# Gate rows built in token pairs instead of token eights (one inference step with a PEER expert mixer)

## Chip, cores and metric

The kernel runs on one core of one Trainium2 chip. The metric is the device time of one execution in microseconds (us), the median of several runs.

## What is computed

One step of a small decoder layer for 512 prompt tokens and 32 sample tokens, 1024 wide: retention heads and a convolution, an output projection, a norm, then PEER, an expert mixer whose experts are single neurons, and a second norm. The part that the change touches is PEER. In the reference it is, for a block of tokens:

```python
v1, i1 = lax.top_k(s1, PEER_TOPK)          # 16 of 128 first keys, per head
v2, i2 = lax.top_k(s2, PEER_TOPK)          # 16 of 128 second keys
cand = v1[..., :, None] + v2[..., None, :]
sv, ci = lax.top_k(cand, PEER_TOPK)        # 16 pairs of keys
e1, e2 = ...                               # first and second key of each pair
idx = e1 * N_KEYS + e2                     # one of 128*128 experts
gate = jax.nn.softmax(sv)
u = jnp.take(peer_u, idx, axis=0)
act = jax.nn.gelu(jnp.einsum('phkd,pd->phk', u, xb), approximate=False)
vv = jnp.take(peer_v, idx, axis=0)
out = jnp.einsum('phk,phkd->pd', gate * act, vv)
```

There are 8 heads with 16 pairs each, so every token chooses 128 of 16,384 experts.

## The kernel before, in words

The tokens are treated in two ways. Some 288 of them (128 prompt tokens at first, the 32 samples, 128 more prompt tokens) **gather** the rows of their experts by indirect DMA: `gather` (L566 to L577) fetches one expert row per token, 128 tokens at a time (1 MB), VectorE multiplies it with the token (L569), ScalarE makes the weight (L571, L572), and VectorE adds the weighted row (L577). The other 256 tokens (`ND`) are treated **densely**: all 128 x 128 experts are scored on TensorE, one second key `e` (128 experts) at a time. `scores_of(e)` loads 512 KB of u and makes eight products, two passes each in the trace (L776, tile `sp`). A table of gates with an entry for every token and expert, most of them zero, is multiplied by the gelu of these scores. `v_stage(e)` then multiplies the result with 512 KB of v into the accumulators `pB` (L907). The table lies in four parts by second key: Gb holds keys 0 to 31, Gc 32 to 51, Ga 52 to 95, Gd 96 to 127 (`EG`, `E0S`).

The table of gates is made by **`build`**, eight tokens (`TB`) to a pass, 256 / 8 = 32 passes to a call. For a token, the partitions are its 128 (head, pair) slots. Matrix A has a one where a slot's first key is `e1`; it is made on ScalarE, per token an absolute difference to a row 0..127 (`off`, L850, eight instructions), then one Relu over the eight tokens (L852). Matrix M has a one where the slot's second key is `e2` (L854, VectorE, one instruction for eight tokens). B is M times the gate of the slot; the gate is split into three bfloat16 parts `gtT[:, q]`, so that B has three parts (L857, one VectorE instruction). For each token three bfloat16 products of A (stationary, 128 columns) and a column set of B (moving, `ne` columns) add up in one PSUM tile: 24 products and 24 weight loads a pass (L863). A result covers `nt` tokens.

`build` is called twice. **`first_keys`** covers the keys 0 to 95 (`ne` = 96, `nt` = 4). For each four tokens VectorE multiplies the PSUM result into Gb and Ga, and into the finished part of Gc (L887), and copies the rest of Gc (L889). In between, `s_stage` scores one key of Gc after every 12 tokens (L871 to L874). **`last_keys`** covers the keys 96 to 127 (`ne` = 32, `nt` = 16); ScalarE copies its result into Gd. It runs later, between the `v_stage`s.

M, B and A have two buffers each, `off` one, the PSUM tiles `mm` and `sp` two each. B is laid out as `[3, ne, TB]`: the eight tokens are innermost, so one token's columns lie 8 elements, 16 bytes, apart:

```python
B = bt.tile([128, 3, ne, TB], BF, name="B")
T.matmul(pt[:, t % nt], A[:, t - t1], B[:, q, :, t - t1], ...)
```

The constant `iot` holds the key numbers, each repeated for the eight tokens, made once by GpSimd at the start (L171).

The order of the instructions on each engine is fixed when the program is built: a scheduler places them by a timeline of its own. Each engine then executes its list in order, and waits on semaphores. In the built order, the 32 passes of `first_keys` stand on TensorE between score products of Gb and Gc: about one key's scores follow each pass, and the last eight passes (192 products) stand without any.

Of the kernel before, what the change touches and what calls it, by code (L numbers as in the profile page):

```python
# [10 lines left out]
BF = mybir.dt.bfloat16  # L11
# [3 lines left out]
OP = mybir.AluOpType  # L15
# [9 lines left out]
PH, NK, TK = 8, 128, 16  # L25
# [6 lines left out]
TB = 8  # L32
# [59 lines left out]
def tile_step(ctx: ExitStack, tc: tile.TileContext, a, o):  # L92
    nc = tc.nc
    V, S, T, G = nc.vector, nc.scalar, nc.tensor, nc.gpsimd

    per = ctx.enter_context(tc.tile_pool(name="per", bufs=1))
# [15 lines left out]
    def mmps():  # L112
        turn[0] += 1
        return banks[turn[0] % len(banks)].tile([128, 512], F32, name="mm")
# [7 lines left out]
    def cc(n):  # L122
        part, c, w = COFF[n]
        return cst[part][:, c:c + w]
# [42 lines left out]
    def small(name, shape, dt=F32, bufs=2):  # L167
        return wk.tile(shape, dt, name=name, bufs=bufs)

    iot = per.tile([128, NK, TB], BF, name="iot")  # L170
    G.iota(iot, pattern=[[1, NK], [0, TB]], base=0, channel_multiplier=0, allow_small_or_imprecise_dtypes=True)  # L171
    row = per.tile([128, NK], BF, name="row")
    G.iota(row, pattern=[[1, NK]], base=0, channel_multiplier=0, allow_small_or_imprecise_dtypes=True)
    mhalf = per.tile([128, 1], F32, name="mhalf")
# [25 lines left out]
    def rope(w, blk, xT, n, col0, outs):  # L200

        def turn_head(h):
            pm = mmps()
            for c0, c1, dst in outs:
                A = dst[:, h]
                T.matmul(pm[:, c0:c1], perm, A, start=True, stop=True)
                B = small("ropeB", [128, 416], bufs=1)[:, :c1 - c0]
                V.tensor_mul(B, pm[:, c0:c1], cc("sin")[:, col0 + c0:col0 + c1])
                V.tensor_mul(A, A, cc("cos")[:, col0 + c0:col0 + c1])
                V.tensor_add(A, A, B)  # L210

# [400 lines left out]
    e2T = per.tile([128, ND], BF, name="e2T")  # L612
    gtT = per.tile([128, 3, ND], BF, name="gtT")
# [183 lines left out]
    for g in range(2):  # L797
# [9 lines left out]
        p = mmps().rearrange("p (q t) -> p q t", q=4)  # L807
# [32 lines left out]
            residual(pB[b][q], x1T, range(q * 4, q * 4 + 4), NG2 + b * 128)  # L840
    GW[1] = gc.tile([128, EG[1], ND], F32, name="Gc")

    def build(bt, e0, ne, nt):


        pt = None
        for t1 in range(0, ND, TB):
            off = bt.tile([128, TB, NK], BF, name="off", bufs=1)
            for t in range(TB):
                S.activation(off[:, t], row, AF.Abs, bias=e1T[:, t1 + t:t1 + t + 1])  # L850
            A = bt.tile([128, TB, NK], BF, name="A")
            S.activation(A, off, AF.Relu, bias=1.0, scale=-1.0)  # L852
            M = bt.tile([128, ne, TB], BF, name="M")
            V.tensor_tensor(M, iot[:, e0:e0 + ne],  # L854
                            e2T[:, t1:t1 + TB].unsqueeze(1).to_broadcast([128, ne, TB]), op=OP.is_equal)
            B = bt.tile([128, 3, ne, TB], BF, name="B")
            V.tensor_tensor(B, M.unsqueeze(1).to_broadcast([128, 3, ne, TB]),  # L857
                            gtT[:, :, t1:t1 + TB].unsqueeze(2).to_broadcast([128, 3, ne, TB]), op=OP.mult)
            for t in range(t1, t1 + TB):
                if t % nt == 0:  # L860
                    pt = pdn.tile([128, nt, ne], F32, name="mm")
                for q in range(3):
                    T.matmul(pt[:, t % nt], A[:, t - t1], B[:, q, :, t - t1], start=(q == 0), stop=(q == 2))  # L863
                if t % nt == nt - 1:
                    yield pt, slice(t - nt + 1, t + 1)

# [9 lines left out]
    def first_keys():  # L876

        with tc.tile_pool(name="bt", bufs=2, reuse_waits="tile") as bt:
            done = 0
            for pt, ts in build(bt, 0, E0S[3], 4):  # L880
                for g, e0, e1, ready in ((0, 0, EG[0], True), (2, 0, EG[2], True), (1, 0, done, True), (1, done, EG[1], False)):
                    if e0 == e1:
                        continue
                    to = GW[g][:, e0:e1, ts]
                    part = pt[:, :, E0S[g] + e0:E0S[g] + e1].rearrange("p t e -> p e t")
                    if ready:
                        V.tensor_mul(to, to, part)  # L887
                    else:
                        V.tensor_copy(to, part)  # L889
                if ts.stop % 12 == 0 and done < EG[1]:  # L890
                    s_stage(E0S[1] + done, ts.stop)
                    done += 1

    def last_keys():

        with tc.tile_pool(name="bt", bufs=2, reuse_waits="tile") as bt:
            for pt, ts in build(bt, E0S[3], EG[3], 16):
                S.activation(GW[3][:, :, ts], pt.rearrange("p t e -> p e t"), AF.Copy)
                yield
# [53 lines left out]
    for b in range(2):  # L953
        t = uvp.tile([128, D], F32, name="uv")
# [50 lines left out]
```

## Time and profile before

| | |
|---|---|
| median of 3 runs | 1742.75 us (1738.49 to 1743.54) |
| profiled execution: its time, its span | 1744.1 us, 1742.3 us |
| mean granted TensorE clock in it | 0.943 |
| busy: TensorE, VectorE, ScalarE, GpSimd | 94%, 72%, 35%, 22% |
| HBM traffic | 503 MB, 289 GB/s over the span |

Busy shares are those of the profiled execution, against its span. A matmul's duration contains its passage through the array, and the next one starts before it ends; the distance from one to the next is what the engine spends on it. Granted clock is the share of full TensorE speed that the chip's throttle gave in that stretch.

### The profile page before, as it was taken

How to read it: one execution, taken by the hardware profiler on the slowest of the kernel's cores; microseconds unless marked ns; L12 is line 12 of the kernel's file. 1: busy time of each engine (PE TensorE's matmuls, PEld its weight loads, DVE VectorE, ACT ScalarE, POOL GpSimd, SP SyncE). 2: the span in 40 equal slices, each digit the busy share in tenths (PEclk: the TensorE clock that was granted, in tenths of full speed). 3: DMA queues.
4: the chain of work that ended last, by engine and by line, in shares of the span. 5: the costliest groups of instructions: out<-in, count | busy, mean ns of one | idle time of the engine just before them, and what ended most of it. 6: DMA issues, size and time to landing. Idle time of an engine off the chain costs nothing.

```text
span 1742.3 us, 20660 instructions
## 1 busy us (share of the span) xinstructions
PE 1635.5 (94%) x7014; PEld 1111.1 (64%) x7014; DVE 1250.1 (72%) x3037; ACT 603.4 (35%) x1687; POOL 375.6 (22%) x335
## 2 busy tenths in 40 slices
PE   7899899969599889999999999999999999999997
PEld 6887566547465578887877666544557665553443
DVE  4949899898658989999566776776665777776201
ACT  1324441452212323334334555541688211111000
POOL 1002222345222222200210110232222422222000
PEclk9899999979799999999998887699999999999998
DMA  9469679978987689955965551499988999999642
GB/s 361 156 211 363 251 257 336 346 266 280 370 322 260 243 317 355 357 190 168 354 251 194 184 202 37 159 415 423 395 291 309 359 424 424 423 424 424 213 154 99
DMA packets 99542, 503.75 MB, mean 289 GB/s; under 512 B 10183, under 2 KB 21191, under 8 KB 56549
## 3 DMA queue, kind: packets, MB, share of 16 engines
q0 software_dynamic: 42240, 305.12, 45.8%
q1 hardware_dynamic: 50749, 189.96, 29.4%
q10 hardware_dynamic: 6448, 7.36, 1.3%
q8 instruction: 55, 0.90, 0.2%
q14 instruction: 50, 0.41, 0.1%
HBM read 497.03 MB, written 5.80 MB: 289 GB/s over the span
## 4 chain that ended last, share of the span: by engine, by line
PE 58%; DVE 21%; DMA 14%; issue 4%; POOL 2%; ACT 1%; SPq 0%; DVEq 0%; POOLq 0%; ACTq 0%
PE pB L907 22%; PE sp L776 15%; PE mm L863 9%; DMA g<-in_uv_dram,I 7%; PE mm L196 5%; DVE acc L577 4%; DVE g L569 4%; PE mm L306 2%; DMA uv<-in_ut_dram 2%; PE mm L261 2%; DMA g<-in_uv_dram,Ib 2%; DMA g<-in_w_in_dram 1%; POOL g L566 1%; DVE oh L546 1%; DMA out_dram<-keys 1%
## 5 line engine op out<-in xcount | busy, mean ns | idle before, releaser
L776 PE MATMUL sp<-x1T,uv 128*128 128x256 f32 x2048 | 485.5, 396 | 19.4 <-ACT Ga L822 7.2
L776 PEld LDWEIGHTS sp<-x1T,uv 128*128 128x128 f32 x2048 | 403.0, 200 | 101.9 <-issue 25.1
L577 DVE SCALAR_TENSOR_TENSOR acc<-g,wgt,acc 128x1024 f32<-128x1024 f32 x285 | 365.1, 1281 | 93.9 <-ACT wgt L572 92.7
L566 POOL DMA_INDIRECT g<-in_uv_dram,I x128 | 167.6, 1310 | 437.3 <-DVE acc L577 228.1
L569 DVE SCALAR_TENSOR_TENSOR g<-g,x1g 128x1024 f32<-128x1024 f32 x160 | 195.3, 1223 | 68.1 <-DMA g<-in_uv_dram,Ib 60.5
L566 POOL DMA_INDIRECT g<-in_uv_dram,Ib x128 | 143.6, 1122 | 406.1 <-DVE acc L577 360.3
L571 ACT ACTIVATE act<-act 128x1 f32<-128x1 f32 x288 | 57.4, 200 | 493.8 <-DVE g L569 493.4
L863 PE MATMUL mm<-B,A 128*128 128x96 bf16 (+1 forms) x1536 | 188.5, 294 | 5.1 <-DVE Gc L889 3.8
L569 DVE SCALAR_TENSOR_TENSOR g<-g,x 128x1024 f32<-128x1024 f32 x128 | 155.8, 1217 | 40.2 <-DMA g<-in_uv_dram,I 38.4
L196 PE MATMUL mm<-x1T,w 128*128 128x384 f32 (+1 forms) x512 | 179.5, 505 | 3.3 <-ACT score L522 2.6
L863 PEld LDWEIGHTS <-A 128*128 128x128 bf16 x1536 | 139.2, 117 | 65.5 <-issue 19.8
L907 PE MATMUL pB<-uv,Ga 128*128 128x512 f32 x352 | 162.3, 604 | 1.1 <-DMA uv<-in_uv_dram 0.8
L850 ACT ACTIVATE off<-row,e1T 128x128 bf16<-128x128 bf16 x512 | 157.8, 388 | 4.0 <-PE mm L863 3.0
L196 PEld LDWEIGHTS mm<-x1T,w 128*128 128x128 f32 x512 | 96.9, 192 | 76.0 <-issue 40.4
L907 PE MATMUL pB<-uv,Gb 128*128 128x512 f32 x256 | 119.9, 622 | 0.4 <-DVE Gb L887 0.4
L907 PEld LDWEIGHTS pB<-uv,Ga 128*128 128x128 f32 x352 | 63.8, 190 | 82.8 <-issue 62.6
L907 PE MATMUL pB<-uv,Gd 128*128 128x512 f32 x256 | 110.1, 593 | 0.1
L852 ACT ACTIVATE A<-off 128x1024 bf16<-128x1024 bf16 x64 | 67.4, 1054 | 97.7 <-PE mm L863 97.3
L907 PEld LDWEIGHTS pB<-uv,Gb 128*128 128x128 f32 x256 | 49.6, 200 | 61.7 <-issue 54.3
L857 DVE TENSOR_TENSOR B<-M,gtT 128x2304 bf16<-128x2304 bf16 (+1 forms) x64 | 60.8, 953 | 38.3 <-PE mm L863 38.3
L907 PEld LDWEIGHTS pB<-uv,Gd 128*128 128x128 f32 x256 | 48.6, 190 | 61.5 <-issue 60.4
L566 POOL DMA_INDIRECT g<-in_uv_dram,Is x32 | 36.0, 1126 | 210.8 <-DVE acc L577 115.5
(277 smaller groups left out, 1787.0 us busy)
## 6 DMA issues: line engine op xcount, KB each, us to landing
uv<-in_ut_dram SPq DMA_DIRECT2D x128, 512.0 KB
uv<-in_uv_dram SPq DMA_DIRECT2D x128, 512.0 KB
w<-in_w_in_dram SPq DMA_DIRECT2D x18, 1024.0 KB
w<-in_w_query_dram SPq DMA_DIRECT2D x16, 1024.0 KB
w<-in_w_out_dram SPq DMA_DIRECT2D x7, 1024.0 KB
g<-in_uv_dram,I POOLq DMA_INDIRECT x128, 7.9
keys<-in_state_retention_dram ACTq DMA_DIRECT2D x4, 512.0 KB
out_dram<-keys SPq DMA_DIRECT2D x4, 512.0 KB
```

Source lines behind the costliest of these rows:

```text
L196: T.matmul(p[:, :n], w[m // 2][:, k, (m % 2) * 128:(m % 2 + 1) * 128], xT[:, k, c0:c0 + n], start=(k == 0), stop=(k == 7))
L261: T.matmul(p[:, :L], dg[:, k % 4], u_p[:, m, p0 + k:p0 + k + L], start=(k == 0), stop=(k == CK - 1))
L566: G.indirect_dma_start(out=t, out_offset=None, in_=a["uv"], in_offset=bass.IndirectOffsetOnAxis(ap=idx[:, k:k + 1], axis=0))
L569: V.scalar_tensor_tensor(t[:, :D], t[:, :D], 1.0, x1, op0=OP.mult, op1=OP.mult, accum_out=act[:, 0:1])
L571: S.activation(act[:, 1:2], act[:, 0:1], AF.Gelu)
L577: V.scalar_tensor_tensor(acc, v, wgt, acc, op0=OP.mult, op1=OP.add)
L776: T.matmul(sp, u[:, k], x1T[:, k, NG2:], start=(k == 0), stop=(k == 7))
L850: S.activation(off[:, t], row, AF.Abs, bias=e1T[:, t1 + t:t1 + t + 1])
L852: S.activation(A, off, AF.Relu, bias=1.0, scale=-1.0)
L857: V.tensor_tensor(B, M.unsqueeze(1).to_broadcast([128, 3, ne, TB]), gtT[:, :, t1:t1 + TB].unsqueeze(2).to_broadcast([128, 3, ne, TB]), op= ...
L863: T.matmul(pt[:, t % nt], A[:, t - t1], B[:, q, :, t - t1], start=(q == 0), stop=(q == 2))
L907: T.matmul(pB[b][q], W[:, b * 128:(b + 1) * 128], vt[:, q * 512:(q + 1) * 512], start=False, stop=(e == NK - 1), skip_group_check=True)
```

## The change

B's layout is cut into pairs of tokens: `[3, TB/2, ne, 2]`, so that one token's columns lie 2 elements, 4 bytes, apart. M gets the same order, `[TB/2, ne, 2]`, and `iot` holds each key number twice instead of eight times. VectorE's one instruction for all three parts of B becomes three, one for each part; its gate operand is now read in runs of two, each repeated for all `ne` keys. The number of elements is the same. `A`, `off`, the weight loads, the count of products, the results and their reading are unchanged. The lines after L842 move down by four: L854 becomes L858, L857 becomes L862, L863 becomes L867, L887 becomes L891.

```diff
-    iot = per.tile([128, NK, TB], BF, name="iot")
-    G.iota(iot, pattern=[[1, NK], [0, TB]], base=0, channel_multiplier=0, allow_small_or_imprecise_dtypes=True)
+    iot = per.tile([128, NK, 2], BF, name="iot")
+    G.iota(iot, pattern=[[1, NK], [0, 2]], base=0, channel_multiplier=0, allow_small_or_imprecise_dtypes=True)
...
+    def pairs_of(x, t1):
+
+        return x[:, t1:t1 + TB].rearrange("p (a b) -> p a b", b=2).unsqueeze(2)
...
-            M = bt.tile([128, ne, TB], BF, name="M")
-            V.tensor_tensor(M, iot[:, e0:e0 + ne],
-                            e2T[:, t1:t1 + TB].unsqueeze(1).to_broadcast([128, ne, TB]), op=OP.is_equal)
-            B = bt.tile([128, 3, ne, TB], BF, name="B")
-            V.tensor_tensor(B, M.unsqueeze(1).to_broadcast([128, 3, ne, TB]),
-                            gtT[:, :, t1:t1 + TB].unsqueeze(2).to_broadcast([128, 3, ne, TB]), op=OP.mult)
+            M = bt.tile([128, TB // 2, ne, 2], BF, name="M")
+            V.tensor_tensor(M, iot[:, e0:e0 + ne].unsqueeze(1).to_broadcast([128, TB // 2, ne, 2]),
+                            pairs_of(e2T, t1).to_broadcast([128, TB // 2, ne, 2]), op=OP.is_equal)
+            B = bt.tile([128, 3, TB // 2, ne, 2], BF, name="B")
+            for q in range(3):
+                V.tensor_tensor(B[:, q], M, pairs_of(gtT[:, q], t1).to_broadcast([128, TB // 2, ne, 2]), op=OP.mult)
...
-                    T.matmul(pt[:, t % nt], A[:, t - t1], B[:, q, :, t - t1], start=(q == 0), stop=(q == 2))
+                    T.matmul(pt[:, t % nt], A[:, t - t1], B[:, q, (t - t1) // 2, :, t % 2], start=(q == 0), stop=(q == 2))
```

## The prediction

> **What bounds the kernel now.** I read the page first, for the engines and the chain of waits.
>
> ```profile
> span 1742.3 us, 20660 instructions
> PE 1635.5 (94%) x7014; PEld 1111.1 (64%) x7014; DVE 1250.1 (72%) x3037; ACT 603.4 (35%) x1687; POOL 375.6 (22%) x335
> ...
> PE 58%; DVE 21%; DMA 14%; issue 4%; POOL 2%; ACT 1%; SPq 0%; DVEq 0%; POOLq 0%; ACTq 0%
> PE pB L907 22%; PE sp L776 15%; PE mm L863 9%; DMA g<-in_uv_dram,I 7%; PE mm L196 5%; DVE acc L577 4%; DVE g L569 4%; PE mm L306 2%; DMA uv<-in_ut_dram 2%; PE mm L261 2%; DMA g<-in_uv_dram,Ib 2%; DMA g<-in_w_in_dram 1%; POOL g L566 1%; DVE oh L546 1%; DMA out_dram<-keys 1%
> ```
>
> TensorE is busy for 94% of the span and carries 58% of the chain; the build's products (L863) are 9% of it. Averages over stages with different limits decide nothing, so next come the stages around `first_keys`: length, then busy time of TensorE, weight loads, VectorE, ScalarE and GpSimd, with counts, then granted clock, DMA share and GB/s.
>
> ```profile
> 845.00:883.00 38.00, 38.00 (x178) 33.36 (x178) 22.82 (x33) 10.85 (x37) 10.45 (x8) 1.00 0.98 377
> 883.00:970.00 87.00, 85.37 (x390) 65.45 (x389) 53.57 (x125) 38.80 (x121) 9.22 (x10) 0.86 0.53 186
> 970.00:1048.00 78.00, 75.91 (x368) 55.16 (x368) 57.03 (x139) 42.47 (x124) 11.46 (x11) 0.82 0.55 196
> 1048.00:1080.00 32.00, 32.00 (x130) 20.93 (x130) 17.42 (x45) 15.59 (x41) 0.79 (x2) 0.80 0.15 50
> 1080.00:1116.00 36.00, 31.85 (x181) 22.15 (x179) 29.96 (x86) 26.08 (x68) 7.29 (x3) 0.51 0.27 92
> 883.00:1116.00 233.00, 225.12 (x1064) 163.69 (x1062) 157.97 (x395) 122.93 (x354) 28.75 (x25) 0.79 0.44 156
> ...
> 1235.00:1320.00 85.00, 85.00 (x590) 52.69 (x589) 53.50 (x86) 70.01 (x201) 20.24 (x16) 1.00 0.88 323
> 1400.00:1500.00 100.00, 97.70 (x327) 59.78 (x326) 72.28 (x94) 18.43 (x67) 25.16 (x27) 1.00 1.02 424
> ```
>
> From 883 to 1116 us TensorE fills 225 of 233 us while DMA runs at 156 GB/s, against 424 later on. VectorE has 158 us of work, ScalarE 123. Only from 1080 on is VectorE (29.96 of 36) nearly as full as TensorE. The same windows for the products of `build` alone, then for the score products alone, show what TensorE does there.
>
> ```profile
> 883.00:970.00 87.00, 38.37 (x216) 24.73 (x214) 0.86 0.53 186
> 970.00:1048.00 78.00, 47.10 (x264) 31.04 (x264) 0.82 0.55 196
> 1048.00:1080.00 32.00, 15.16 (x86) 10.02 (x86) 0.80 0.15 50
> 1080.00:1116.00 36.00, 31.85 (x181) 22.15 (x179) 0.51 0.27 92
> 883.00:1116.00 233.00, 132.48 (x744) 87.94 (x742) 0.79 0.44 156
> ...
> 883.00:970.00 87.00, 49.75 (x174) 40.72 (x175) 0.86 0.53 186
> 970.00:1048.00 78.00, 29.82 (x99) 23.14 (x98) 0.82 0.55 196
> 1048.00:1080.00 32.00, 10.03 (x32) 7.98 (x32) 0.80 0.15 50
> 883.00:1116.00 233.00, 89.59 (x304) 71.83 (x304) 0.79 0.44 156
> ```
>
> 744 of the 768 products of the 96-key build lie here, at 132.48 / 744 = 178 ns each. So 57% of the stage is spent on these products alone.
>
> **Why they cost 178 ns.** From the chain in order of time (start, length):
>
> ```profile
> 131.96 7.15 PE mm L196 x64
> 844.98 37.99 PE sp L776 x176
> 1098.90 16.81 PE mm L863 x96
> 1266.26 2.88 PE mm L863 x48
> ```
>
> At 1098.90, 96 products with 96 columns take 175 ns each; at 1266.26, with 32 columns, 60 ns. That is 1.8 ns a column both times, nearly without a fixed part, and the first comes where the clock is granted at 0.51, the second at 1.00: what limits it does not follow the clock. The float32 score products read columns 4 bytes apart: 37.99 / 176 = 216 ns for 256 columns, 0.84 ns a column, in a stretch at clock 1.00. The one difference in the reading is the step: 16 bytes in `build`, 4 there. The 128-column float32 products at 131.96 follow each other at 112 ns with their own 128-column weight loads, so a load hides behind a product.
>
> **Part 1: products at 4 bytes' step.** The new price is bounded above by the float32 rate, 96 x 0.84 = 81 ns, and below by 60 ns, the cheapest product with the same weight load in this trace. I take 65, nearer the row with the same load and type. Of each 178 ns 113 go: 24.3 us in the first window (216 x 0.113), 29.9, 9.7 and 20 in the others. TensorE is left with 61, 46, 22 and 12 us: 141 for 225.
>
> The row says step, not why. [...]
>
> The 32-column products of `last_keys` already stand at 60 ns; no row shows a cheaper pair, so I take nothing there.
>
> **Part 2: VectorE pays.** One B of 2304 elements becomes three of 768; M keeps its 768 elements, read differently. The rows of both builds (the second B and the second M are `last_keys`'), the nearest row that reads single repeated elements, and two starts from the chain in order of time:
>
> ```profile
> L857 DVE TENSOR_TENSOR B<-M,gtT 128x2304 bf16<-128x2304 bf16 x32 | 43.1, 1349 | 1.4 <-PE mm L863 1.4
> L857 DVE TENSOR_TENSOR B<-M,gtT 128x768 bf16<-128x768 bf16 x32 | 17.8, 558 | 36.9 <-PE mm L863 36.9
> L854 DVE TENSOR_TENSOR M<-iot,e2T 128x768 bf16<-128x768 bf16 x32 | 17.5, 552 | 0.0
> L854 DVE TENSOR_TENSOR M<-iot,e2T 128x256 bf16<-128x256 bf16 x32 | 8.7, 288 | 0.3
> L546 DVE TENSOR_TENSOR oh<-row,pf 128x800 bf16<-128x800 bf16 x34 | 33.5, 984 | 0.1
> ...
> 1085.27 1.26 DVE B L857
> 1086.54 0.47 DVE M L854
> ```
>
> 2304 elements take 1349 ns and 768 take 558: (1349 - 558) / 1536 = 0.52 ns an element. In `oh` one operand repeats a single element, and 800 take 984 ns, about double. No row reads runs of two. Lower bound: the starts in the chain, 3 x 0.47 - 1.26 = +0.15 us a pass. Middle: 3 x 0.558 - 1.349 = +0.33. Upper: all four instructions at the `oh` price, 768 / 800 x 984 = 945 ns, so 4 x 0.945 - 1.349 - 0.552 = +1.88. I take +0.33, since a run of two is still a run of neighbours, as the present runs of eight are, and keep the upper end as a rival.
>
> [...]
>
> The first three windows hold 9, 11 and 3.6 passes, the last 7.5 (products / 24). VectorE rises from 53.6, 57.0, 17.4, 30.0 to 56.5, 60.7, 18.6, 32.4 us, some of it now queued ahead of the multiplications of Gb and Ga (L887), for which the PSUM tile waits. In `last_keys` three of 256 replace one of 768; M's row of that size gives 3 x 288 - 558 = +0.31 us a pass, 10 us in all, under TensorE (85.00 of 85 busy in 1235 to 1320, VectorE 53.50). Without that cover it would be those 10 us.
>
> **Part 3: what is late next.** The largest engine in each window, after parts 1 and 2: 61 (TensorE; VectorE 56.5), 60.7 (VectorE), 22 (TensorE), 32.4 (VectorE). Sum 176. Two engines that are nearly equal and wait for each other do not fill a window: TensorE alone now leaves 8 of 233 us, and VectorE's waits on it are many:
>
> ```profile
> L887 DVE TENSOR_TENSOR Gb<-Gb,mm 128x128 f32<-128x128 f32 x64 | 18.3, 285 | 71.9 <-PE mm L863 69.5 <-ACT Gb L827 1.8
> ```
>
> These 69.5 us are the room that VectorE has; most of it goes. I add 8 us as now: 184 for 233, a gain of 49, and 1 us for the 24 products before 883. ScalarE makes A unchanged, and stays below VectorE's 168 us:
>
> ```profile
> L850 ACT ACTIVATE off<-row,e1T 128x128 bf16<-128x128 bf16 x512 | 157.8, 388 | 4.0 <-PE mm L863 3.0
> L852 ACT ACTIVATE A<-off 128x1024 bf16<-128x1024 bf16 x64 | 67.4, 1054 | 97.7 <-PE mm L863 97.3
> ```
>
> (157.8 + 67.4) / 64 = 3.5 us a pass, where a pass will last 184 / 31 = 5.9 us; its 97.3 us of waits on L863 are room.
>
> After 1116 the order is as before. TensorE fills 97.7 of 100 us from 1400 to 1500 and DMA runs at 424 GB/s; both streams begin where `first_keys` ends, so they should shift whole. The stage's 36 MB (233 us x 156 GB/s) in 184 us make 198 GB/s, far from 424. GpSimd's `iota` gets four times smaller at the start, with nobody waiting. TensorE's, SyncE's and ScalarE's queues are handed no new wait; VectorE's list gets 128 instructions.
>
> Sum: 1744.1 (the profiled execution, span 1742.3 plus 1.8) - 50 = 1694.1. The median shown, 1742.75, lies 1.35 lower; 50 from it is 1692.8. Forecast **1693 us**.
>
> **Rivals.**
>
> *The clock falls.* Where TensorE waits, the clock is granted at 0.51 (1080 to 1116). With a VectorE-bound stage this could spread. Score products cost 49.75 / 174 = 286 ns at clock 0.86 against 216 at 1.00. Half the clock would double 216 to 432, but a full TensorE does not idle; I take the middle, 359, and 120 (double 60) for the build's product. The first window then holds 174 x 0.359 + 216 x 0.12 = 88 us, no gain; the second 35.5 + 31.7 = 67, a gain of 11; the third, with its 6.8 us of other products, 11.5 + 10.3 + 6.8 = 29, a gain of 3; the last as before. Fourteen in all: 1730. Against it: 1235 to 1320 mixes such short products with long ones at clock 1.00, and the dense products should raise the load seen. [...]
>
> *The clock recovers and the engines interleave well.* If VectorE alone bounds the stage at 158 + 31 x 0.15 = 163 us, 70 go, with 2 more before 883: 1671.
>
> *The step isn't the reason.* Were 178 ns the price of 96 bfloat16 columns with this weight load for another reason, only VectorE's +5 to +10 us would remain, under TensorE: 1743 to 1748. The 1.8 ns a column, whatever the clock, speak against it.
>
> *Pairs are slow on VectorE (the slower side).* The four products of a pass cost 1.9 us now. VectorE has 158 / 31 = 5.1 us of work a pass, and a pass lasts 233 / 31 = 7.5, so from 4.3 us for the four on it is the later engine. At the `oh` price (3.8) the windows need 70, 78, 24 and 44 us, 216 and 8 of waits, a gain of 9: about 1735. At 4.5 us, a penalty for short runs on top, a pass needs 5.1 - 1.9 + 4.5 = 7.7, and 31 x 7.7 + 8 = 247, 14 more than now: 1758. No row shows such a penalty.
>
> **How the numbers follow.** Forecast as above (gain 30 to 62) 0.62; fuller gain, near 1671, 0.11; the clock, 1730, 0.06; longer waits between the engines than 8 us, with a gain of 10 to 30, 0.06; step not the reason 0.06; slow pairs 0.09 (0.02 of it at the `oh` price, taken as even). The range leaves out the slow pairs, the step not being the reason, and half of the fuller gains, 0.2 in all: from 1670, VectorE's floor, to 1735, past the clock's case. A difference of 0.3% (5.2 us) is about what can be told from no change. Faster 0.85; same 0.07; slower 0.08.
>
> **What would show it.** Right: the 96-column products 60 to 81 ns apart; the stage of the 96-key build near 184 us; VectorE over 85% busy in it, its waits at L891 on L867 far below 69.5; B's new rows at about 558 ns, M's unchanged. Wrong: products still near 178 ns, B's rows near 945 ns, or the clock near 0.5 with score products over 300 ns.

## The result, and the profile after

The kernel with pairs takes 1647.95 us in the median of four runs (1644.09 to 1653.35); the kernel before 1740.62, beside it. The ratio is 0.9473, 95% interval 0.9435 to 0.951: 92.7 us less. A second series of the same kernel gave 1651.19 against 1741.24, 0.9472 (0.9442 to 0.9501). The forecast was 1693 us, in a range from 1670 to 1735. The sign was right, the size half of what came, and the time lies outside the range.

The page after, its first lines and its chain:

```profile
span 1642.3 us, 20790 instructions
PE 1505.7 (92%) x7014; PEld 1021.4 (62%) x7014; DVE 1254.3 (76%) x3165; ACT 601.2 (37%) x1687; POOL 386.2 (24%) x335
...
PE 49%; DVE 27%; DMA 14%; issue 5%; ACT 3%; POOL 2%; SPq 0%; DVEq 0%; POOLq 0%; ACTq 0%
```

TensorE has lost 130 us of work and 9 points of the chain, VectorE has gained 6 points. To place the loss in time, the first and last start of two instructions mark the two builds: the multiplication into Gb for the 96-key build, the copy into Gd for the 32-key build. Before, after, and then a second profiled execution of each (duration min/median/max, first and last start):

```profile
L887 DVE TENSOR_TENSOR Gb<-Gb,mm x64: 267/288/291, 880.0 to 1115.7; 128x128 f32<-128x128 f32 x64
L898 ACT ACTIVATE Gd<-mm x16: 574/597/597, 1231.0 to 1362.7; 128x512 f32<-128x512 f32 x16
```

```profile
L891 DVE TENSOR_TENSOR Gb<-Gb,mm x64: 222/281/296, 867.8 to 1033.3; 128x128 f32<-128x128 f32 x64
L902 ACT ACTIVATE Gd<-mm x16: 572/578/597, 1151.3 to 1260.5; 128x512 f32<-128x512 f32 x16
```

```profile
L887 DVE TENSOR_TENSOR Gb<-Gb,mm x64: 267/288/290, 864.5 to 1100.2; 128x128 f32<-128x128 f32 x64
L898 ACT ACTIVATE Gd<-mm x16: 581/597/598, 1214.9 to 1348.3; 128x512 f32<-128x512 f32 x16
```

```profile
L891 DVE TENSOR_TENSOR Gb<-Gb,mm x64: 222/276/289, 871.9 to 1038.7; 128x128 f32<-128x128 f32 x64
L902 ACT ACTIVATE Gd<-mm x16: 571/578/597, 1156.3 to 1265.3; 128x512 f32<-128x512 f32 x16
```

The 96-key build takes 235.7 us before, both times, and 165.5 and 166.8 after: 70 less. The 32-key build takes 131.7 and 133.4 before and 109.2 and 109.0 after: 23 less. Together that is the 93 us. Where the 96-key build starts (880.0 and 864.5 for one and the same kernel) varies from one execution to the next; that is why the first two profiled executions are 100 us apart and the second two 82, where the medians differ by 92.7.

The two stages after (columns as in the prediction's windows), and the build's products alone in the first:

```profile
868.00:1034.00 166.00, 129.56 (x1078) 109.01 (x1078) 161.67 (x464) 122.40 (x355) 34.92 (x26) 0.83 0.65 231
1004.00:1034.00 30.00, 16.04 (x181) 14.06 (x182) 29.01 (x100) 24.03 (x62) 10.89 (x5) 0.53 0.34 110
1150.00:1262.00 112.00, 111.31 (x928) 65.14 (x927) 83.85 (x181) 102.31 (x297) 34.81 (x26) 1.00 0.96 367
...
868.00:1034.00 166.00, 48.69 (x744) 43.81 (x744) 0.83 0.65 231
```

In the first, VectorE now works 161.67 of 166 us and TensorE idles for 36; in the second TensorE still fills 111.31 of 112. The build's 744 products went from 132.48 us to 48.69. The rows that replace those of the prediction:

```profile
L867 PE MATMUL mm<-B,A 128*128 128x96 bf16 x768 | 50.2, 228 | 32.3 <-DVE Gc L893 31.4 <-DVE Gc L891 0.9
L862 DVE TENSOR_TENSOR B<-M,gtT 128x768 bf16<-128x768 bf16 x96 | 47.6, 550 | 0.0
L858 DVE TENSOR_TENSOR M<-iot,e2T 128x768 bf16<-128x768 bf16 x32 | 17.5, 549 | 0.1
L891 DVE TENSOR_TENSOR Gb<-Gb,mm 128x128 f32<-128x128 f32 x64 | 17.8, 279 | 5.2 <-PE mm L867 3.4 <-ACT Gb L827 1.8
```

The wait has changed sides. VectorE waited 69.5 us for TensorE's products at L887; now 3.4 at L891, and TensorE waits 31.4 us for VectorE's last reading of a PSUM tile (L893).

### The profile page after: what moved, and what is told of

Read it like the earlier page. It is cut to its first block, busy times and chain, and to the rows that moved or that the text cites. A ratio compares the mean times of both kernels' runs of the same rounds, so it can differ in the third digit from the quotient of the medians.

```text
span 1642.3 us, 20790 instructions
## 1 busy us (share of the span) xinstructions
PE 1505.7 (92%) x7014; PEld 1021.4 (62%) x7014; DVE 1254.3 (76%) x3165; ACT 601.2 (37%) x1687; POOL 386.2 (24%) x335
## 4 chain that ended last, share of the span: by engine, by line
PE 49%; DVE 27%; DMA 14%; issue 5%; ACT 3%; POOL 2%; SPq 0%; DVEq 0%; POOLq 0%; ACTq 0%
PE pB L911 23%; PE sp L776 10%; PE mm L196 7%; DVE acc L577 5%; DMA g<-in_uv_dram,I 5%; DVE g L569 5%; PE mm L306 2%; DVE B L862 2%; DMA uv<-in_ut_dram 2%; PE mm L261 2%; DMA uv<-in_uv_dram 2%; DMA g<-in_w_in_dram 2%; DMA g<-in_uv_dram,Is 1%; PE mm L867 1%; DVE pick L549 1%
## 5 line engine op out<-in xcount | busy, mean ns | idle before, releaser
L776 PE MATMUL sp<-x1T,uv 128*128 128x256 f32 x2048 | 473.7, 388 | 19.6 <-ACT Ga L822 8.6
L776 PEld LDWEIGHTS sp<-x1T,uv 128*128 128x128 f32 x2048 | 389.4, 194 | 97.6 <-issue 26.1
L566 POOL DMA_INDIRECT g<-in_uv_dram,I x128 | 163.6, 1278 | 433.7 <-DVE acc L577 221.3
L566 POOL DMA_INDIRECT g<-in_uv_dram,Ib x128 | 155.8, 1217 | 387.1 <-DVE acc L577 255.2
L854 ACT ACTIVATE off<-row,e1T 128x128 bf16<-128x128 bf16 x512 | 157.8, 389 | 2.8 <-PE mm L867 1.9
L867 PE MATMUL mm<-B,A 128*128 128x96 bf16 (+1 forms) x1536 | 74.5, 202 | 36.5 <-DVE Gc L893 31.4
L867 PEld LDWEIGHTS <-A 128*128 128x128 bf16 x1536 | 69.0, 103 | 61.0 <-issue 34.1
L862 DVE TENSOR_TENSOR B<-M,gtT 128x768 bf16<-128x768 bf16 (+1 forms) x192 | 69.4, 418 | 8.6 <-PE mm L867 8.5
```

The lines of the kernel that those rows point to most:

```text
L566: G.indirect_dma_start(out=t, out_offset=None, in_=a["uv"], in_offset=bass.IndirectOffsetOnAxis(ap=idx[:, k:k + 1], axis=0))
L776: T.matmul(sp, u[:, k], x1T[:, k, NG2:], start=(k == 0), stop=(k == 7))
L862: V.tensor_tensor(B[:, q], M, pairs_of(gtT[:, q], t1).to_broadcast([128, TB // 2, ne, 2]), op=OP.mult)
L867: T.matmul(pt[:, t % nt], A[:, t - t1], B[:, q, (t - t1) // 2, :, t % 2], start=(q == 0), stop=(q == 2))
```

## The experiments

**Each build alone.** A build with a free group size `g`, and with B in one VectorE instruction or three, was called as

```diff
-            for pt, ts in build(bt, 0, E0S[3], 4):
+            for pt, ts in build(bt, 0, E0S[3], 4, 2, False):    # 96 keys: pairs, three instructions
-            for pt, ts in build(bt, E0S[3], EG[3], 16):
+            for pt, ts in build(bt, E0S[3], EG[3], 16, 8, True):  # 32 keys: eights, one instruction
```

> Pairs in the 96-key build alone; the 32-key build keeps eights. Theory A (each build gains by the price of its own products: the 96-key stage becomes VectorE's, 236 to about 166 us, and the 32-key stage gains 22 us because its products fall from 60 to 25 ns): the first part of the gain alone, about 1670 us, with the 32-key stage at its old 131 us and its products at 60 ns. Rival B (the 32-key stage gained from its earlier start or its order, not from the price): about 1648, 32-key stage near 110 us with products still at 60 ns.

Measured: 1670.48 us, ratio 0.9594 (0.9574 to 0.9615), 71.9 us less. With the two calls' groups exchanged:

> Pairs in the 32-key build alone. Theory A: 32-key products at 25 ns, that stage 131 to about 110 us, the 96-key stage unchanged at 236 us: about 1718 us. Rival B: no gain, 1741 us within 5.

Measured: 1713.11 us, ratio 0.9847 (0.9817 to 0.9877), 29.2 us less. The products in the two kernels, first pairs for 96 keys, then pairs for 32:

```profile
L874 PE MATMUL mm<-B,A 128*128 128x32 bf16 x768 | 50.9, 237 | 0.7 <-ACT Gd L909 0.7
L874 PE MATMUL mm<-B,A 128*128 128x96 bf16 x768 | 49.4, 226 | 34.0 <-DVE Gc L900 31.4 <-ACT A L859 1.3 <-DVE Gc L898 0.9
```

```profile
L874 PE MATMUL mm<-B,A 128*128 128x96 bf16 x768 | 137.3, 350 | 3.7 <-DVE Gc L900 3.7
L874 PE MATMUL mm<-B,A 128*128 128x32 bf16 x768 | 24.5, 177 | 3.2 <-DVE B L869 2.0 <-ACT Gd L909 0.7 <-ACT A L859 0.4
```

In each kernel the products read in pairs are busy for about half the time or less (49.4 us against 137.3, 24.5 against 50.9), and the others keep their price. The marks of the two builds, first with pairs for 96 keys, then with pairs for 32, show the stages:

```profile
L898 DVE TENSOR_TENSOR Gb<-Gb,mm x64: 220/276/289, 872.9 to 1041.0; 128x128 f32<-128x128 f32 x64
L909 ACT ACTIVATE Gd<-mm x16: 582/597/598, 1155.0 to 1286.7; 128x512 f32<-128x512 f32 x16
```

```profile
L898 DVE TENSOR_TENSOR Gb<-Gb,mm x64: 222/287/290, 866.2 to 1102.5; 128x128 f32<-128x128 f32 x64
L909 ACT ACTIVATE Gd<-mm x16: 570/579/597, 1216.6 to 1326.5; 128x512 f32<-128x512 f32 x16
```

That is 168.1 and 131.7 us, then 236.3 and 109.9: each stage gains by its own products' price, and the other stage stays. The two gains in the medians add up to 101 us, somewhat over the 92.7 of both (by the ratios 97 against 92); the intervals (some 4, 5 and 6 us to a side) about cover that.

**VectorE's side alone**: eights in both builds, B in three instructions (`g` = 8, three).

> Eights as before, but B made by three VectorE instructions in both builds: VectorE's side of the change without TensorE's. Theory A: products stay at 178 and 60 ns, VectorE's extra 5 to 10 us in each build hide under TensorE: 1741 to 1748 us. Rival C (part of the gain comes from splitting B, whose first third is ready earlier): 1725 us or less.

Measured: 1740.24 us, ratio 0.9981 (0.9959 to 1.0003). Splitting B costs nothing while TensorE sets the stage, and brings nothing.

**The step between 16 and 4 bytes, and below**: `g` = 4 (a token's columns 8 bytes apart), and then `g` = 1 (2 bytes), in both builds.

> [...] If the price is in proportion to the step: 89 ns and 30 ns, TensorE 66 us of products beside 81 of scores in the 96-key stage, still under VectorE's 162: about 1650 to 1665 us. If every step over 4 bytes costs the old price: 178 and 60 ns and 1741 us.

Measured: 1661.02 us, ratio 0.9543 (0.9515 to 0.9572).

> Groups of one token in both builds: a token's columns next to each other (2 bytes), VectorE's second operand repeats single elements. [...] VectorE: if only a run of two or more keeps the double rate, M and B cost about 945 ns each in place of 550, +1.6 us a pass, and the 96-key stage, VectorE's, grows from 166 to about 216: 1698 us within 8. If single elements keep the double rate as well: 1648 us.

Measured: 1700.08 us, ratio 0.9761 (0.9718 to 0.9804). The products in the chain in order of time (start, length), of the kernel after (32 columns), then of the fours (96 and 32 columns):

```profile
1193.20 1.19 PE mm L867 x48
```

```profile
906.90 2.08 PE mm L872 x24
1192.08 1.53 PE mm L872 x48
```

A product of 32 columns costs 1.19 / 48 = 25 ns with pairs, 1.53 / 48 = 32 with fours, and 60 with eights; one of 96 columns 2.08 / 24 = 87 with fours. With pairs and with singles the starts in the timeline give the 96-column price at full clock: from the first product to the score product that follows the last, of the kernel after and then of the singles,

```profile
899.94 1.20 PE L867 MATMUL mm<-B,A 128*128 128x96 bf16 x24
900.98 4.11 PE L776 MATMUL sp<-x1T,uv 128*128 128x256 f32 x18
```

```profile
884.00 1.18 PE L872 MATMUL mm<-B,A 128*128 128x96 bf16 x24
885.02 3.69 PE L777 MATMUL sp<-x1T,uv 128*128 128x256 f32 x16
```

(900.98 - 899.94) / 24 = 43 ns, and 1.02 / 24 = 43 ns. The clock granted in the first of these stretches was 1.00; after the fours' and the singles' products the score products follow at 217 ns (26 from 908.80 to 914.45) and 220 ns (16 from 885.02 to 888.54), where the prediction has 216 at clock 1.00. So at full clock a column of the 96-column products costs 1.8 ns at 16 bytes' step, 0.9 at 8, 0.45 at 4 and 0.45 at 2: in proportion to the step, down to a floor that is reached at 4. The proportional rule of the expectation held (89 and 30 ns against 87 and 32). Why the price goes with the step, no run shows.

Singles have the same products and lose 52 us against pairs. The reason is on VectorE:

```profile
L867 DVE TENSOR_TENSOR B<-M,gtT 128x768 bf16<-128x768 bf16 x96 | 85.7, 944 | 0.0
L859 DVE TENSOR_TENSOR M<-iot,e2T 128x768 bf16<-128x768 bf16 x32 | 30.1, 944 | 0.0
...
877.00:1096.00 219.00, 141.68 (x1077) 116.27 (x1075) 208.38 (x463) 122.22 (x355) 42.89 (x27) 0.78 0.50 178
```

An operand of repeated single elements costs 944 ns where pairs cost 550, VectorE's work in the stage rises to 208 us, and the stage to 219. Pairs are thus the one grouping tried in which both engines have their better price. The fours lose 13 us against pairs although VectorE's work in the 96-key stage is the pairs' (161.77 us); that stage, then the products alone:

```profile
871.00:1051.00 180.00, 152.83 (x1080) 130.90 (x1078) 161.77 (x461) 121.83 (x354) 27.00 (x25) 0.87 0.60 210
...
871.00:1051.00 180.00, 70.25 (x744) 64.27 (x744) 0.87 0.60 210
```

The products take 22 us more than with pairs (70.25 against 48.69), and the stage some 13 us more.

**What sets the 96-key stage now.** First VectorE, with one instruction more a pass:

```diff
             V.tensor_tensor(M, iot[...]..., pairs_of(e2T, t1)..., op=OP.is_equal)
+            if ne == E0S[3]:
+                V.tensor_tensor(M, iot[...]..., pairs_of(e2T, t1)..., op=OP.is_equal)
```

> Pairs, and M of the 96-key build made twice: one more VectorE instruction of 0.47 us a pass, start to start, result unchanged. Theory A (VectorE sets the 96-key stage): 31 x 0.47 = 15 us more, stage 166 to 181, 1663 us within 4. Rival (the waits between the engines set it and VectorE has room): 1648 us within 4.

Measured: 1658.67 us, ratio 0.955 (0.9514 to 0.9586); the stage lasts 176.3 us, 9.5 to 10.8 more than in the two executions with M made once, not the 15 expected. Then TensorE, with all products of the stage doubled:

```diff
-                for q in range(3):
+                for q in [0, 1, 2] * (2 if nt == 4 else 1):
                     T.matmul(pt[:, t % nt], ..., start=(q == 0), stop=(q == 2))
```

> Pairs, and the 24 products of each pass of the 96-key build made twice, the second set starting anew: 744 more products of 43 ns at full clock, 32 us more TensorE work in the stage, result unchanged. Theory A (VectorE sets the stage, TensorE has 36 of 166 us free): most is hidden, stage 166 to 170 to 180, 1650 to 1662 us. Rival (TensorE or its latency still sets the stage): 32 us or more, 1680 us or later.

Measured: 1662.35 us, ratio 0.9571 (0.9536 to 0.9606); the stage lasts 173.5 us. The two stages in windows, M twice and then products twice:

```profile
870.00:1047.00 177.00, 129.61 (x1072) 107.17 (x1070) 173.34 (x489) 122.96 (x353) 37.79 (x26) 0.84 0.59 215
```

```profile
867.00:1041.00 174.00, 145.69 (x1812) 128.52 (x1811) 161.75 (x463) 121.90 (x353) 30.32 (x26) 0.98 0.60 219
```

M twice adds 11.7 us to VectorE's work (from 161.67) and about 10 to the stage, nearly one for one. The doubled products add 16 us to TensorE's work (from 129.56; 744 x 43 ns would be 32, but the granted clock rises from 0.83 to 0.98, and the 2048 score products get cheaper, 468.6 us in all for 473.7) and 7 to 8 us to the stage: about half of it shows, as with the fours. The median, 1662.35, lies at the upper edge of what Theory A allowed. So VectorE's work sets most of the stage, and TensorE's is only in part hidden behind it. The rise of the clock with more work (0.98 with 145.69 us of it, 0.83 with 129.56) shows that the low clock is not the result of too much work. Whether it comes from idle time is not shown: in the kernel before, TensorE was counted busy for 32.00 of 32 us (1048 to 1080 in the prediction's windows) at a clock of 0.80.

**Taking work off VectorE.** The copies of Gc's unfinished part on ScalarE, and then one of B's three multiplications on GpSimd:

```diff
                     else:
-                        V.tensor_copy(to, part)
+                        S.activation(to, part, AF.Copy)
```

> Pairs, and the copies of the unfinished part of Gc in the 96-key stage (62 of them, 0.08 to 0.16 us start to start on VectorE) made by ScalarE instead. Theory A: VectorE loses about 7 us of the 162 that set the stage, ScalarE rises from 122 to about 137 of 160 us: 1641 us within 4. Rival (ScalarE's copies wait for TensorE in front of the rows of A, and these come late): 1648 us or more.

Measured: 1653.88 us, ratio 0.9513 (0.9485 to 0.9541).

```diff
             for q in range(3):
-                V.tensor_tensor(B[:, q], M, ...)
+                (G if ne == E0S[3] and q == 2 else V).tensor_tensor(B[:, q], M, ...)
```

> Pairs, and the third part of B in the 96-key build (one of three multiplications, 768 elements) made by GpSimd instead of VectorE. If VectorE's load alone sets the stage and GpSimd's instruction takes up to about 3 us of a pass of 5.3: 31 x 0.47 = 15 us come off VectorE, stage 166 to about 153, 1636 us within 5. Rival: GpSimd is slower than that, or holds up the issue of gathers behind it, or slows VectorE beside it: stage 166 or longer, 1648 us or more.

Measured: 1662.87 us, ratio 0.9558 (0.9529 to 0.9587). Both expected gains failed to come, and neither kernel beats the kernel after (0.9473). The products and the stage in the first, then the 96-key build's GpSimd and VectorE rows and the stage in the second:

```profile
L867 PE MATMUL mm<-B,A 128*128 128x96 bf16 x768 | 49.1, 227 | 30.3 <-ACT Gc L893 30.1
...
868.00:1046.00 178.00, 134.17 (x1079) 111.13 (x1077) 157.08 (x403) 126.30 (x415) 34.47 (x26) 0.83 0.59 216
```

```profile
L862 POOL TENSOR_TENSOR B<-M,gtT 128x768 bf16<-128x768 bf16 x32 | 61.2, 1912 | 46.5 <-PE mm L867 35.4 <-DVE M L858 4.4 <-DVE g L569 3.2
L862 DVE TENSOR_TENSOR B<-M,gtT 128x768 bf16<-128x768 bf16 x64 | 40.1, 666 | 0.0
L858 DVE TENSOR_TENSOR M<-iot,e2T 128x768 bf16<-128x768 bf16 x32 | 22.5, 705 | 0.2
...
870.00:1050.00 180.00, 133.09 (x1070) 109.59 (x1068) 174.04 (x423) 119.82 (x349) 84.82 (x55) 0.84 0.61 214
```

With the copy on ScalarE, VectorE has less work, 157 us, and yet the stage lasts 177.5 us: VectorE now idles for 21 us of it in place of 4. It waits 11 us for TensorE's products (3 before) and 11 for gathered rows (1 and 2 in the two executions with pairs). TensorE's wait for the last reading of a PSUM tile is no longer than before, 30.1 us on ScalarE's copy against 31.4 on VectorE's. Which of ScalarE's delays holds the others up stays open. With a third on GpSimd, VectorE has 32 instructions fewer and yet more busy time, 174.04 us: its own instructions beside GpSimd's take 666 and 705 ns in place of 550. The stage lasts 179.8 us.

**The second profiles** of both kernels, whose rows stand in the first section:

> The changed kernel once more, beside the others of this call. 1648 us within 4; first multiplication of Gb at 868 us within 4, that stage 166 us, the 32-key stage 109 us, if the profile of after was typical.

> The kernel before once more, for a second profile. If its later start of the 96-key stage (first multiplication of Gb at 880 us, against 866 to 873 in all the others) belongs to that one execution: 866 to 874 now. If it belongs to the order that the scheduler made for this kernel: 880 within 3 again, and some 10 us of the gain are the order's.

Measured: 1651.19 us and, in its one execution, 1729.59. The kernel before started its 96-key stage at 864.5 this time, so the order does not fix the start at 880.

## Why the prediction was wrong in size

Measured were 92.7 us less, forecast 50. Of the 43 missing, 23 are the 32-key stage, which Part 1 put at nothing, and 20 the 96-key stage, which Part 3 made too long.

**The mechanism held.** The step was the reason for the 178 ns, the stage was TensorE's, TensorE's gain met VectorE as the next limit, and what follows the two builds (114.7 to 118 us between them, 380 to 382 behind them) only moved forward.

**Part 1, the floor, is the step that failed.** I took 60 ns, the price of the 32-column products, as the cheapest that a pair of load and product can be, and wrote that `last_keys` gains nothing. But those products read at the same 16 bytes' step. The prediction's own line, 1.8 ns a column both times and nearly no fixed part, gives 32 x 1.8 = 58 ns: the row was the limit at work, not a floor below it. They fell to 25 ns, 768 x 35 ns = 27 us of TensorE work; 672 of the products lie between the stage's two marks, 24 us in a stage that TensorE fills, and it became 23 us shorter.

For the 96 columns the assumed 65 ns was right on the mean (48.69 us / 744 = 65) by luck: the mean mixes 43 ns at full clock with twice that at half, and the sign "60 to 81 ns apart" was met at neither. The lower bound of 60 was the same wrong floor. The upper bound of 81, from the float32 rate, was exceeded at half clock only; it was no measure of the step alone, as the prediction said, for at the same 4 bytes a bfloat16 column costs 0.45 ns where a float32 column cost 0.84. At the stage's end, where 0.53 was granted (the window 1004 to 1034 above), the chain of the kernel after has

```profile
1031.20 2.09 PE mm L867 x24
```

which is 87 ns a product.

**Part 3, the stage's length,** was 184 us and came to 166, in the range of the rival "the engines interleave well" (163). Three terms were too large. VectorE's added price: I took durations, +0.33 us a pass, 10 us in all; B's rows in the page, 43.1 us before and 47.6 after for 32 passes, give +0.14, since the instructions overlap (96 of 550 ns would be 52.8 us), as the lower bound (+0.15, starts in the chain) had it. VectorE's busy time in the whole stage was 160.16 us in the second profile of before and 161.67 after. The windows: I took the later engine in each and added up, 8 us more than VectorE alone, and in two of them let TensorE, at its old clock and 65 ns, be the later one; it was not. The waits: I added 8 us, and VectorE idles 4. The stage in the second profile of before, for comparison:

```profile
864.00:1100.00 236.00, 228.34 (x1081) 166.44 (x1079) 160.16 (x401) 123.37 (x356) 31.11 (x25) 0.79 0.45 160
```

**Part 2 held otherwise:** pairs keep the price that runs of eight have, 550 ns for the forecast's 558; singles do not (944). That a run of two would keep it was an estimate, from the runs of eight. In the 32-key build VectorE's extra instructions stayed under TensorE, as said.

**The rivals.** "The clock falls" did not decide: 0.83 in the stage against 0.79 before, with TensorE idle. "Step isn't the reason" and "slow pairs" are refuted by the fours and by the 550 ns. "The clock recovers and the engines interleave well", 1671, was nearest; it lacks just the 23 us of `last_keys`, and the range ended there because the floor of Part 1 stood below every case. Only its second half came: the clock hardly recovered (0.79 to 0.83).

## What to carry to other kernels

Before a row is used as a floor, ask whether the limit that is about to go acts in that row as well: two rows with the same price per column and no fixed part may both be set by it. Where a stage changes hands, compare its length with the next engine's work summed over the whole stage, at start-to-start prices: with pairs, with M twice, with singles and with a third on GpSimd the stage was 4 to 11 us longer than VectorE's work. It is no more than a lower bound, though: with fours and with ScalarE's copies the stage was 18 and 21 us longer. And work moved off an engine can cost more than it saves, here by VectorE's waits (ScalarE: 21 us idle for 4) or by its own slower instructions (GpSimd: 666 and 705 ns for 550).

## What the runs showed of the hardware

- TensorE's price for a strided bfloat16 operand goes with the step, in products of 96 columns at full clock: 1.8, 0.9, 0.45 and 0.45 ns a column at 16, 8, 4 and 2 bytes (eights, fours, pairs, singles); with eights a product of 96 columns took 171 ns at full clock (24 of them from 901.17 to 905.27) and 175 where only 0.51 of the clock was granted, while the pairs' 43 ns went to 87 where 0.53 was.
- Products of 32 columns, each with a weight load of 128 columns, follow each other at 25 ns with pairs (48 in 1.19 us, in a stage at clock 1.00).
- A GpSimd multiplication of 768 bfloat16 elements takes 1.9 us (1912 ns on the mean of 32), and VectorE's instructions in the same stage rise, B's from 550 to 666 ns, M's from 549 to 705.
